# Adding DMAs for a weight sum only in the second and third part of each FFN, and another choice of groups with four pairs in seven products

## The chip, the cores and the metric

The kernel runs on one core of a Trainium2 chip, as one launch. Its time is the device time of that core in microseconds; of several runs the median is given. The engines are named as in the profile: PE (TensorE matmul) and PEld (its weight loads), DVE (VectorE), ACT (ScalarE), POOL (GpSimd) and SP (SyncE, which issues most of the DMAs).

## The reference

A decoder trunk of two layers over 256 positions of width 2048, all in float32. Each layer is a mixer and an FFN:

```python
for layer in range(DEPTH):
    xn = rms_norm(h, norm_mix[layer])
    mix = swa_mlstm_mixer(xn, ...) if layer % 2 == 0 else forgetting_attention_mixer(xn, ...)
    h = h + mix
    h = h + swiglu(rms_norm(h, norm_ffn[layer]), w_gate[layer], w_up[layer], w_down[layer])
return rms_norm(h, norm_final)

def swiglu(xn, w_gate, w_up, w_down):
    return (jax.nn.silu(xn @ w_gate) * (xn @ w_up)) @ w_down
```

The change is in `swiglu` alone: w_gate and w_up are 2048 x 5632, w_down is 5632 x 2048.

## The kernel before

**Products in halves.** A float32 weight chunk is split in two parts, `hi` (ACT casts it to fp32r) and `lo` (DVE: raw minus hi). So is the left side (`xh`, `xl` for the normed stream, `mh`, `ml` for the hidden values). A product is then three matmuls: hi with xh, lo with xh, hi with xl (`three`, lines 532 to 534). One weight chunk is 256 rows by 512 columns, 128 x 1024 in a tile.

**The FFN's walk.** The 5632 hidden columns are 11 groups of 512 (g = 0 to 10), in three parts: groups 0 to 2, 3 to 6 and 7 to 10 (`PARTS`). For each group `pair_group` computes the gate and the up columns together, over 16 blocks of 128 rows taken as eight pairs. When a part's groups are done, two further calls of `pair_group` multiply the hidden values of that part by w_down, two column blocks of 512 each (in the last part of the second FFN one such call, and two plain products).

**A pair in eight or in seven products.** For a pair of row blocks, two row tiles of positions and two matrices (gate and up) there are eight block products, 24 matmuls. That is a plain pair (kind 0 in the order tables). A pair of kind 1 is computed by a scheme with seven products, 21 matmuls, at the price of sums: of the left side (`sums_of`, made once and kept) and of the weights, which are made for every pair. The second matrix's first row block gets the first matrix's added to it; DVE then subtracts twice (lines 605 and 607), and ACT and DVE split four tiles instead of two (lines 187 and 188 for the raw gate chunk, 356 and 357 for the sums). At a group's end `combine` (lines 555 to 559) puts the four extra accumulators together.

`ORDER` has three pairs of kind 1 among eight, `HEAVY` has four (pairs 1, 3, 5 and 7, where pair 7 is `FOURTH`). A group whose number is in `DENSE` takes `HEAVY`. The down passes have two such pairs of six in part one (`DOWN[6]`) and three of eight in the others (`DOWN[8]`).

**Who makes the first sum.** The tile `ra` gets the gate chunk and `rb` the up chunk, by two plain DMAs that SP issues. The sum is then made by an adding DMA that POOL issues: it reads the same 128 x 512 of w_gate (in a down pass, of w_down's first column block) from memory once more and adds it to `rb` on the way in (line 599). It has to wait until the up chunk has landed; ACT's cast of `rb` (line 356) waits for it. `rb` and `ra` come from a pool of five tiles (`RAWS`), plain chunks from another one of four; the split parts go through eight pairs of tiles (`stock`), which PE empties.

**What sets the order.** The program is built by a planner that places the instructions of each engine by its own estimate of times; each engine then runs its own list strictly in that order. `run_due` puts some work at fixed places of a group: the copies that turn the normed residual stream for group 0 (`split_turned`, its `join` is line 322) and those that turn a group's hidden values (lines 703 and 710).

Of the kernel before, what the change touches and what calls it, by code (L numbers as in the profile page):

```python
# [12 lines left out]
ALU = mybir.AluOpType  # L13
# [10 lines left out]
NB = 512  # L24
# [11 lines left out]
ORDER = ((0, 0), (1, 1), (0, 2), (1, 3), (0, 4), (1, 5), (0, 6), (0, 7))  # L36
HEAVY = ((1, 1), (0, 0), (1, 3), (0, 2), (1, 5), (0, 4), (1, 7), (0, 6))
FOURTH = 7
DENSE = (1, 4, 5, 8, 9)
DOWN = {  # L40
    6: ((0, 0), (1, 1), (0, 2), (1, 3), (0, 4), (0, 5)),
    8: ((0, 0), (1, 1), (0, 2), (1, 3), (0, 4), (1, 5), (0, 6), (0, 7)),
# [33 lines left out]
def trunk(  # L76
# [19 lines left out]
    nc = tc.nc  # L96
# [58 lines left out]
    for n in (1, 2, 3):  # L155
# [8 lines left out]
        out=ident, in_=ident, pattern=[[-1, P]], compare_op=ALU.not_equal, fill=1.0, base=0, channel_multiplier=1  # L164
# [73 lines left out]
    sums = {}  # L238
# [116 lines left out]
    def split_plain(dst_h, dst_l, src):  # L355
        nc.scalar.copy(dst_h, src)  # L356
        nc.vector.tensor_tensor(out=dst_l, in0=src, in1=dst_h.bitcast(F32), op=ALU.subtract)  # L357
# [178 lines left out]
    def bank(par, name):  # L536
        return pm.tile([P, NB], F32, tag="pm", name=name) if par else pa.tile([P, NB], F32, tag="acc", name=name)

    def pair_group(fp, par, lhs, sums, mats, order, todo=(), halves=None, inner=None, raws=None):
        plain = [[bank(par, "acc") for _ in range(NT)] for _ in range(2)]  # L540
        begun = set()

        def fresh(*at):
            known = at in begun
            begun.add(at)
            return not known

        todo = list(todo)
        prods = None
        kinds = [kind for kind, _ in order]  # L550
        t0, t1 = slice(0, P), slice(P, 2 * P)

        def combine(prods):
            c = fp.tile([P, 4, NB], F32, tag="c", name="c", bufs=1)
            nc.scalar.copy(c[:, 0, :], prods[0])
            if halves is None:
                nc.vector.tensor_tensor(out=c[:, 1, :], in0=prods[3], in1=c[:, 0, :], op=ALU.add)
                nc.vector.tensor_tensor(out=c[:, 2, :], in0=prods[2], in1=c[:, 1, :], op=ALU.add)
                nc.vector.tensor_tensor(
                    out=c[:, 1:4:2, :],  # L560
                    in0=prods[1].rearrange("p (a n) -> p a n", a=1).broadcast_to([P, 2, NB]),
                    in1=c[:, 1:3, :],
                    op=ALU.subtract,
                )
                return c
            nc.vector.tensor_tensor(out=c[:, 2, :], in0=prods[3], in1=c[:, 0, :], op=ALU.add)
            nc.vector.tensor_tensor(out=c[:, 1, :], in0=prods[2], in1=c[:, 2, :], op=ALU.add)
            nc.vector.tensor_tensor(out=c[:, 3, :], in0=prods[1], in1=c[:, 1, :], op=ALU.subtract)
            nc.vector.tensor_tensor(out=c[:, 2, :], in0=prods[1], in1=c[:, 2, :], op=ALU.subtract)
            return c  # L570

        for pos, (kind, pair) in enumerate(order):
            k0 = 2 * pair
            if inner is not None and pos == len(order) - 1:
                c = combine(prods)
                inner()
            if not kind:
                last = pos == len(order) - 1
                walk = [(i, t) for i in range(CK) for t in range(NT)]
                if last:  # L580
                    walk.sort(key=lambda it: it[1])
                for m, (w, c0) in enumerate(mats):
                    hi, lo = load_chunk(w, k0, c0, NB)
                    run_due(todo, pos)
                    for i, t in walk:
                        ah, al = lhs(k0 + i)
                        ts = slice(t * P, (t + 1) * P)
                        three(
                            plain[m][t], ah[:, ts], al[:, ts], hi[:, i, :], lo[:, i, :],
                            fresh(m, t), last and i == CK - 1,  # L590
                        )
                continue
            first, last = 1 not in kinds[:pos], 1 not in kinds[pos + 1 :]
            if first:
                prods = [bank(1 - par, "prod") for _ in range(4)]
            ra, rb = (load_raw(w, k0, c0, NB, fp, W_RAWS if halves else RAWS, raws) for w, c0 in mats)
            if halves is None:
                (w, c0), part = mats[0], slice(k0 * P, (k0 + 1) * P)
                nc.gpsimd.dma_start(rb[:, 0, :], w[part, c0 : c0 + NB], accum_op=ALU.add)  # L599
            hg, lg = split_chunk(ra, NB)  # L600
            run_due(todo, pos)
            hu, lu = slot()
            if halves is None:
                split_plain(hu, lu, rb)
                nc.vector.tensor_tensor(out=rb[:, 1, :], in0=rb[:, 0, :], in1=rb[:, 1, :], op=ALU.subtract)  # L605
                both = rb[:, 1, :].rearrange("p (a n) -> p a n", a=1).broadcast_to([P, CK, NB])
                nc.vector.tensor_tensor(out=ra, in0=ra, in1=both, op=ALU.subtract)  # L607
                hc, lc = (a[:, 0, :] for a in slot())
                split_plain(hc, lc, rb[:, 1, :])
                hd, ld = slot()  # L610
                split_plain(hd, ld, ra)
                ht = [hu[:, 0, :], hd[:, 0, :], hc, hd[:, 1, :]]
                lt = [lu[:, 0, :], ld[:, 0, :], lc, ld[:, 1, :]]
            else:
                split_plain(hu[:, 1, :], lu[:, 1, :], rb[:, 1, :])
                nc.vector.tensor_tensor(out=ra[:, 0, :], in0=rb[:, 0, :], in1=ra[:, 0, :], op=ALU.add)
                nc.vector.tensor_tensor(out=rb[:, 0, :], in0=rb[:, 1, :], in1=rb[:, 0, :], op=ALU.subtract)
                nc.vector.tensor_tensor(out=rb[:, 1, :], in0=ra[:, 0, :], in1=rb[:, 1, :], op=ALU.subtract)
                nc.vector.tensor_tensor(out=ra[:, 1, :], in0=ra[:, 1, :], in1=rb[:, 1, :], op=ALU.subtract)
                parts = []  # L620
                for src in (ra, rb):
                    hs, ls = halves.pop(0)
                    halves.append((hs, ls))
                    split_plain(hs, ls, src)
                    parts.append((hs, ls))
                where = ((0, 0), (1, 0), (1, 1), (0, 1))
                ht = [parts[a][0][:, b, :] for a, b in where]
                lt = [parts[a][1][:, b, :] for a, b in where]
            sh, sl = sums(pair)
            xa, la = lhs(k0)  # L630
            xb, lb = lhs(k0 + 1)
            three(prods[0], xa[:, t0], la[:, t0], hg[:, 0, :], lg[:, 0, :], first, last)
            three(plain[0][0], xb[:, t0], lb[:, t0], hg[:, 1, :], lg[:, 1, :], fresh(0, 0), False)
            three(plain[1][0], sh[3], sl[3], hu[:, 1, :], lu[:, 1, :], fresh(1, 0), False)
            three(prods[1], sh[0], sl[0], ht[0], lt[0], first, last)
            three(prods[2], sh[2], sl[2], ht[1], lt[1], first, last)
            three(prods[3], sh[1], sl[1], ht[2], lt[2], first, last)
            three(plain[0][1], xb[:, t1], lb[:, t1], ht[3], lt[3], fresh(0, 1), False)
        if inner is None:
            c = combine(prods)  # L640
        return plain, c

    def ffn(layer, fp, sx, x4, sd, key, todo, idx_next=None, key_next=None, finish=None):
# [8 lines left out]
        for g0, g1 in zip(PARTS, PARTS[1:]):  # L652
            end = g1 == PARTS[-1]
            nk = 4 * (g1 - g0)
            order = DOWN[nk // 2]
            for g in range(g0, g1):
                par = (g1 - 1 - g) % 2
# [5 lines left out]
                    [(w_gate[layer], g * NB), (w_up[layer], g * NB)],  # L663
                    HEAVY if g in DENSE else ORDER,
                    todo,
                )
                todo = []
                for m in range(2):
# [79 lines left out]
            for n0 in (0, 2):  # L748
                if end and idx_next is None and n0 == 2:
                    for n in (2, 3):  # L750
                        acc = new_acc()
                        gemm(acc, m_of, wd, n * NB, NB, 0, nk, nk, skew=3 if n == 3 else 1, halved=n == 3)
                        close(acc, n)
                    continue
                plain, c = pair_group(
                    fp, 1 - n0 // 2, m_of, sums_d, [(wd, n0 * NB), (wd, (n0 + 1) * NB)], order, todo
                )
                todo = []
                if end and idx_next is None:
                    gf = fp.tile([P, D], F32, tag="c", name="gf", bufs=1)  # L760
                    nc.gpsimd.dma_start(gf, norm_final.partition_broadcast(P))
                for t in range(NT):
                    o = h[:, t, n0 * NB : (n0 + 2) * NB]
                    nc.vector.tensor_tensor(
                        out=o, in0=c[:, 2 * t : 2 * t + 2, :].rearrange("p a n -> p (a n)"), in1=o, op=ALU.add
                    )
                for m in range(2):
                    close(plain[m], n0 + m)
# [614 lines left out]
```

## Time and profile before

| | |
|---|---|
| median of 3 runs | 2097.1 us (2096.4 to 2097.92) |
| the profiled execution, its own time | 2095.33 us |
| its span, first to last instruction | 2093.6 us |
| busy: PE / PEld / DVE / ACT / POOL | 99% / 82% / 86% / 66% / 6% |
| mean granted clock of PE | 0.998 |
| adding DMAs (line 599) | 76 from w_gate, 29 from w_down, 256 KB each |
| DMA traffic | 462.43 MB, mean 221 GB/s |

Time before and after the span belongs to the launch. A row of a group reads: line, engine, operation, output<-inputs, count, busy time in us, mean ns of one, then the idle time of the engine just before these instructions and what ended most of it. Matmuls overlap, so a busy PE is not a PE at its full pace; how many matmuls a stretch held for its length tells more. In a table by stretch each engine has its busy time and, in brackets, how many instructions it began there; then come PE's granted clock, the DMA engines' busy share and GB/s.

### The profile page before, as it was taken

To read this page: it belongs to the slowest core of one execution; us is meant where nothing else is said; L and a number is where in the kernel's file an instruction comes from. 1 tells how busy PE (TensorE), PEld (TensorE's weight loads), DVE (VectorE), ACT (ScalarE), POOL (GpSimd) and SP (SyncE) were. 2 spreads that over 40 slices of the span, in tenths; PEclk is the share of its full clock that TensorE was granted. 3 is DMA by queue.
4 is the path that set the end of the run, shared out by engine and by line. 5 is a ranking of instruction groups with operands and counts; after the bars stand their busy time and mean duration, and the time that the engine had idled before them with its cause. 6 is when DMAs were issued, how large, how long until landed. Compare 5 with 4: busy or idle time off the path is not lost.

```text
span 2093.6 us, 27094 instructions
## 1 busy us (share of the span) xinstructions
PE 2072.1 (99%) x9443; PEld 1709.8 (82%) x9443; DVE 1794.4 (86%) x2217; ACT 1384.1 (66%) x1764; POOL 133.7 (6%) x171
## 2 busy tenths in 40 slices
PE   9999999999999999999999999999999999999998
PEld 8878887778888888888888888887788888888887
DVE  6788768988999998998899678578899999999995
ACT  6767677665567656667676776686655667557763
POOL 1010000000000000000000001000000000000000
PEclk9999999999999999999999999999999999999999
DMA  8666578777788777887676777597778777867864
GB/s 294 177 201 201 195 257 226 217 215 218 220 229 265 227 244 220 237 238 202 204 225 198 227 201 186 162 263 202 243 220 244 228 223 234 265 201 209 263 208 150
DMA packets 324698, 462.43 MB, mean 221 GB/s; under 512 B 108092, under 2 KB 116304, under 8 KB 324432
## 3 DMA queue, kind: packets, MB, share of 16 engines
q1 hardware_dynamic: 307088, 426.27, 64.8%
q0 software_dynamic: 16752, 33.33, 9.0%
q8 instruction: 74, 1.21, 0.2%
q10 hardware_dynamic: 720, 1.09, 0.1%
q14 instruction: 64, 0.52, 0.1%
HBM read 436.21 MB, written 2.12 MB: 209 GB/s over the span
## 4 chain that ended last, share of the span: by engine, by line
PE 75%; DVE 8%; DMA 6%; ACT 5%; issue 4%; SPq 0%; ACTq 0%; POOLq 0%; POOL 0%; DVEq 0%
PE acc L533 16%; PE acc L532 16%; PE acc L534 16%; PE prod L533 4%; PE prod L532 4%; PE prod L534 4%; PE acc L222 4%; PE acc L223 4%; PE acc L224 4%; DVE lo L188 2%; DVE lo L357 2%; DMA raw<-in_w_down_dram 2%; ACT hi L187 2%; DMA raw<-in_w_gate_dram 1%; ACT hi L356 1%
## 5 line engine op out<-in xcount | busy, mean ns | idle before, releaser
L188 DVE TENSOR_TENSOR lo<-raw,hi 128x1024 fp32r<-128x1024 f32 (+2 forms) x646 | 761.7, 1194 | 153.8 <-ACT hi L187 151.2
L187 ACT CAST hi<-raw 128x1024 fp32r<-128x1024 f32 (+2 forms) x646 | 651.6, 1026 | 319.8 <-PE acc L534 83.7
L533 PE MATMUL acc<-lo,xh 128*128 128x512 f32 x1260 | 491.7, 391 | 1.0 <-DVE lo L188 1.0
L534 PE MATMUL acc<-hi,xl 128*128 128x512 f32 x1260 | 490.1, 390 | 0.0
L532 PE MATMUL acc<-hi,xh 128*128 128x512 f32 x1260 | 478.6, 392 | 5.5 <-ACT hi L187 3.9
L356 ACT CAST hi<-raw 128x1024 fp32r<-128x1024 f32 (+1 forms) x329 | 291.4, 894 | 226.5 <-DVE raw L605 84.6
L357 DVE TENSOR_TENSOR lo<-raw,hi 128x1024 fp32r<-128x1024 f32 (+1 forms) x329 | 334.9, 1029 | 52.2 <-ACT hi L356 50.8
L532 PEld LDWEIGHTS acc<-hi,xh 128*128 128x128 f32 x1260 | 236.8, 188 | 58.8 <-ACT hi L187 7.7
L533 PEld LDWEIGHTS acc<-lo,xh 128*128 128x128 f32 x1260 | 236.8, 188 | 53.0 <-DVE lo L188 3.9
L534 PEld LDWEIGHTS acc<-hi,xl 128*128 128x128 f32 x1260 | 236.9, 188 | 48.9
L533 PE MATMUL acc<-lo,mh 128*128 128x512 f32 x466 | 181.6, 390 | 0.0
L534 PE MATMUL acc<-hi,ml 128*128 128x512 f32 x466 | 181.4, 389 | 0.0
L532 PE MATMUL acc<-hi,mh 128*128 128x512 f32 x466 | 175.8, 390 | 0.5 <-ACT hi L187 0.5
L607 DVE TENSOR_TENSOR raw<-raw 128x1024 f32<-128x1024 f32 x105 | 128.3, 1222 | 1.0
L599 POOL DMA_DIRECT2D raw<-in_w_gate_dram x76 | 65.1, 856 | 963.9 <-DMA raw<-in_w_up_dram 391.4
L223 PE MATMUL acc<-lo,mh 128*128 128x512 f32 (+1 forms) x322 | 126.3, 392 | 0.0
L222 PE MATMUL acc<-hi,mh 128*128 128x512 f32 (+1 forms) x322 | 125.8, 391 | 0.0
L224 PE MATMUL acc<-hi,ml 128*128 128x512 f32 (+1 forms) x322 | 123.7, 391 | 0.0
L532 PEld LDWEIGHTS acc<-hi,mh 128*128 128x128 f32 x466 | 87.5, 188 | 19.4 <-ACT hi L187 1.3
L533 PEld LDWEIGHTS acc<-lo,mh 128*128 128x128 f32 x466 | 87.5, 188 | 18.1
L534 PEld LDWEIGHTS acc<-hi,ml 128*128 128x128 f32 x466 | 87.5, 188 | 18.1
L223 PE MATMUL acc<-lo,xh 128*128 128x512 f32 (+3 forms) x288 | 99.7, 347 | 0.2 <-DVE lo L188 0.2
(361 smaller groups left out, 3093.3 us busy)
## 6 DMA issues: line engine op xcount, KB each, us to landing
raw<-in_w_gate_dram SPq DMA_DIRECT2D x176, 512.0 KB, 5.2
raw<-in_w_up_dram SPq DMA_DIRECT2D x176, 512.0 KB, 5.4
raw<-in_w_down_dram SPq DMA_DIRECT2D x176, 512.0 KB, 5.7
raw<-in_w_in_odd_dram SPq DMA_DIRECT2D x88, 512.0 KB, 5.3
raw<-in_w_in_even_dram SPq DMA_DIRECT2D x51, 512.0 KB, 4.8
raw<-in_w_gate_dram POOLq DMA_DIRECT2D x76, 256.0 KB, 5.7
raw<-in_w_out_even_dram SPq DMA_DIRECT2D x32, 512.0 KB, 5.4
raw<-in_w_out_odd_dram SPq DMA_DIRECT2D x32, 512.0 KB, 4.8
```

The source lines that it names most:

```text
L187: latest[0] = nc.scalar.copy(hi[:, k, 0:n], raw[:, k, 0:n])
L188: nc.vector.tensor_tensor(out=lo[:, k, 0:n], in0=raw[:, k, 0:n], in1=hi[:, k, 0:n].bitcast(F32), op=ALU.subtract)
L222: nc.tensor.matmul(o, ah[:, ts], hi, start=(k == 0), stop=False)
L223: nc.tensor.matmul(o, ah[:, ts], lo, start=False, stop=False)
L224: nc.tensor.matmul(o, al[:, ts], hi, start=False, stop=(k == k_all - 1 and cs.stop == n))
L356: nc.scalar.copy(dst_h, src)
L357: nc.vector.tensor_tensor(out=dst_l, in0=src, in1=dst_h.bitcast(F32), op=ALU.subtract)
L532: nc.tensor.matmul(o, ah, hi, start=start, stop=False)
L533: nc.tensor.matmul(o, ah, lo, start=False, stop=False)
L534: nc.tensor.matmul(o, al, hi, start=False, stop=stop)
L599: nc.gpsimd.dma_start(rb[:, 0, :], w[part, c0 : c0 + NB], accum_op=ALU.add)
L607: nc.vector.tensor_tensor(out=ra, in0=ra, in1=both, op=ALU.subtract)
```

## The change

In both FFNs:

- Part one (groups 0 to 2 and their down pass) has no adding DMA any more. DVE makes the sum, one 128 x 512 add of `ra` to `rb`, ahead of the split of `rb`. It reads two tiles that the plain DMAs fill. Parts two and three keep the adding DMA.
- Group 1 goes back to three pairs in seven products, and groups 3 and 7, the first ones of parts two and three, get four. So three groups with four such pairs follow each other in each of these parts: 3, 4, 5 and 7, 8, 9.

Counted over the kernel, 105 adding DMAs become 81, and 26 adds on DVE come. 28 adding DMAs leave part one (per FFN ten in the groups and four in the down pass), four come to parts two and three.

```diff
-DENSE = (1, 4, 5, 8, 9)
+DENSE = (3, 4, 5, 7, 8, 9)
+ADDING = 3
...
-    def pair_group(fp, par, lhs, sums, mats, order, todo=(), halves=None, inner=None, raws=None):
+    def pair_group(fp, par, lhs, sums, mats, order, todo=(), halves=None, inner=None, raws=None, adding=False):
...
             ra, rb = (load_raw(w, k0, c0, NB, fp, W_RAWS if halves else RAWS, raws) for w, c0 in mats)
-            if halves is None:
+            if adding:
                 (w, c0), part = mats[0], slice(k0 * P, (k0 + 1) * P)
                 nc.gpsimd.dma_start(rb[:, 0, :], w[part, c0 : c0 + NB], accum_op=ALU.add)
             hg, lg = split_chunk(ra, NB)
             run_due(todo, pos)
             hu, lu = slot()
             if halves is None:
+                if not adding:
+                    nc.vector.tensor_tensor(out=rb[:, 0, :], in0=ra[:, 0, :], in1=rb[:, 0, :], op=ALU.add)
                 split_plain(hu, lu, rb)
...
                     HEAVY if g in DENSE else ORDER,
                     todo,
+                    adding=g0 >= ADDING,
...
-                    fp, 1 - n0 // 2, m_of, sums_d, [(wd, n0 * NB), (wd, (n0 + 1) * NB)], order, todo
+                    fp, 1 - n0 // 2, m_of, sums_d, [(wd, n0 * NB), (wd, (n0 + 1) * NB)], order, todo, adding=g0 >= ADDING
```

Lines behind the change move down by one to four: 187, 322, 356 and 357 become 188, 323, 357 and 358; 599 becomes 600; the new add is 606, and 605 and 607 become 608 and 610; 671 and 675 become 675 and 679.

The planner's order changes with it. First POOL's list over the first FFN; `r` is the norm's factor and `st` work of the mixer before. Before:

```order
L1108 TENSOR_TENSOR st<-st,mhalf 128x2 x4
L599 DMA raw<-in_w_gate_dram 128x512 x3
L254 TENSOR_TENSOR r<-tot,mhalf 128x2
L599 DMA raw<-in_w_gate_dram 128x512 x7
L599 DMA raw<-in_w_down_dram 128x512 x4
L599 DMA raw<-in_w_gate_dram 128x512 x14
```

After:

```order
L1112 TENSOR_TENSOR st<-st,mhalf 128x2 x4
L255 TENSOR_TENSOR r<-tot,mhalf 128x2
L600 DMA raw<-in_w_gate_dram 128x512 x15
L600 DMA raw<-in_w_down_dram 128x512 x6
L600 DMA raw<-in_w_gate_dram 128x512 x15
```

The ten and four of part one are gone from POOL, and each later part has 15 instead of 14.

Next ACT's list in group 0 of the first FFN, around the copies that turn the last quarter of the normed stream (`box`); `hi_3096` and the like are fixed split tiles of `stock`. Before:

```order
L361 ACTIVATE xh<-box,gT 128x256 x4
L303 ACTIVATE full<-box,gT 128x256 x2
L187 COPY hi<-raw 128x1024 x3
L322 COPY box<-box 128x1024 x2
L356 COPY hi<-raw 128x512
L356 COPY hi<-raw 128x1024 x2
```

After:

```order
L362 ACTIVATE xh<-box,gT 128x256 x4
L304 ACTIVATE full<-box,gT 128x256 x2
L188 COPY hi<-raw 128x1024 x2
L357 COPY hi<-raw 128x512
L188 COPY hi<-raw 128x1024
L323 COPY box<-box 128x1024 x2
L357 COPY hi<-raw 128x1024 x2
```

The 128x512 cast of the sums (line 356, now 357) has moved ahead of the copies.

Last DVE's list at the end of group 0 and the start of group 1, from the sums of group 0's results (line 671, now 675) on. Before:

```order
L671 TENSOR_TENSOR c<-acc,c 128x512 x3
L357 TENSOR_TENSOR lo<-raw,hi 128x512
L607 TENSOR_TENSOR raw<-raw 128x1024
L675 TENSOR_SCALAR c<-c,r 128x512
L357 TENSOR_TENSOR lo<-raw,hi 128x1024
L188 TENSOR_TENSOR lo<-raw,hi 128x1024
```

After:

```order
L675 TENSOR_TENSOR c<-acc,c 128x512 x3
L608 TENSOR_TENSOR raw<-raw 128x512
L189 TENSOR_TENSOR lo<-raw,hi 128x1024
L679 TENSOR_SCALAR c<-c,r 128x512
L189 TENSOR_TENSOR lo<-raw,hi 128x1024
L610 TENSOR_TENSOR raw<-raw 128x1024
L358 TENSOR_TENSOR lo<-raw,hi 128x512
L679 TENSOR_SCALAR c<-c,r 128x512
L358 TENSOR_TENSOR lo<-raw,hi 128x1024 x2
L608 TENSOR_TENSOR raw<-raw 128x512
L606 TENSOR_TENSOR raw<-raw 128x512
L610 TENSOR_TENSOR raw<-raw 128x1024
```

The add of a pair (line 606) stands in DVE's list among the subtractions of the pair before it, with splits of other chunks behind it.

## The prediction

> **What bounds the kernel now.** I read the page first, then the busy time of each engine stretch by stretch, then the waits of PE and ACT in the stretches that stood out, and last single instructions there.
>
> ```profile
> span 2093.6 us, 27094 instructions
> ...
> PE 2072.1 (99%) x9443; PEld 1709.8 (82%) x9443; DVE 1794.4 (86%) x2217; ACT 1384.1 (66%) x1764; POOL 133.7 (6%) x171
> ...
> PE 75%; DVE 8%; DMA 6%; ACT 5%; issue 4%; SPq 0%; ACTq 0%; POOLq 0%; POOL 0%; DVEq 0%
> ```
>
> PE is the bound, DVE the next engine. In the chain that ended last 23% is not PE (8 + 6 + 5 + 4), so the question is where PE is fed late. The six stretches below are the gate/up groups of part one, two and three of the first FFN, then of the second; PEld counts the weight loads, one for each matmul.
>
> ```profile
> core 0: us, PE busy (x) PEld busy (x) DVE busy (x) ACT busy (x) POOL busy (x), PEclk, DMA share, GB/s
> 321.70:457.50 135.80, 131.46 (x556) 104.31 (x555) 116.88 (x145) 96.43 (x119) 9.27 (x11) 0.99 0.78 222
> 519.80:684.30 164.50, 164.50 (x727) 136.29 (x726) 155.93 (x176) 109.79 (x121) 11.95 (x14) 1.00 0.80 235
> 767.30:932.60 165.30, 164.89 (x727) 136.08 (x726) 153.85 (x174) 109.36 (x120) 11.95 (x14) 1.00 0.79 234
> 1388.20:1526.00 137.80, 132.31 (x556) 103.88 (x555) 117.23 (x146) 96.77 (x119) 9.28 (x11) 0.99 0.79 219
> 1588.10:1752.70 164.60, 164.60 (x728) 136.29 (x727) 153.86 (x173) 109.60 (x120) 11.95 (x14) 1.00 0.80 235
> 1835.70:2000.20 164.50, 164.50 (x727) 136.24 (x726) 153.46 (x172) 109.15 (x120) 11.95 (x14) 1.00 0.80 235
> ```
>
> Parts two and three run at 164.5 / 726 = 0.2266 us a matmul, and three of the four have no gap in PE at all. At that pace the 555 of part one would take 125.8 us. They take 135.8 and 137.8: **10.0 and 12.0 us lost, 22.0 in all**. Only 0.8 us is lost elsewhere in the FFN groups (165.3 against 164.5). Single groups of part one, with a group of each kind from the later parts:
>
> ```profile
> 321.70:365.40 43.70, 42.88 (x185) 33.96 (x184) 34.82 (x50) 34.30 (x50) 3.28 (x4) 1.00 0.82 222
> 365.40:411.90 46.50, 44.12 (x182) 34.75 (x181) 41.72 (x48) 32.64 (x36) 3.43 (x4) 0.96 0.76 218
> 411.90:457.50 45.60, 44.46 (x193) 35.59 (x192) 40.34 (x48) 29.49 (x34) 2.56 (x3) 1.00 0.76 226
> ```
> ```profile
> 849.60:891.20 41.60, 41.19 (x182) 33.58 (x181) 40.88 (x48) 29.49 (x34) 3.43 (x4) 1.00 0.86 256
> 519.80:561.30 41.50, 41.50 (x185) 34.38 (x184) 40.20 (x43) 24.30 (x27) 3.40 (x4) 1.00 0.75 228
> 561.30:602.10 40.80, 40.80 (x182) 33.80 (x181) 37.26 (x44) 28.87 (x32) 2.56 (x3) 1.00 0.74 217
> 457.50:519.80 62.30, 62.02 (x278) 51.03 (x277) 55.77 (x59) 32.19 (x37) 3.43 (x4) 1.00 0.74 221
> ```
>
> Group 0 loses 43.7 − 184 × 0.2266 = 2.0 us, group 1 (four pairs in seven products) 46.5 − 41.0 = 5.5, group 2 45.6 − 43.5 = 2.1. A group of the same form as group 1 takes 40.8 in part two (561.3). DVE is not full in part one (116.88 of 135.8), so something makes it wait. ACT's waits in part one, first FFN and then second:
>
> ```profile
> ACT hi L356 <- DMA raw<-in_w_gate_dram: 11.1, 2, 5.8
> ...
> ACT hi L187 <- DMA raw<-in_w_up_dram: 1.6, 1, 1.6
> ```
> ```profile
> ACT hi L356 <- DMA raw<-in_w_gate_dram: 9.0, 2, 5.7
> ...
> ACT hi L187 <- DMA raw<-in_w_up_dram: 3.0, 2, 2.3
> ```
>
> L356 casts the tile `rb`, whose plain load comes from w_up; what reaches it from w_gate is the adding DMA alone. So 20.1 us of ACT's waiting here is for adding DMAs, against 4.6 for the loads. One of them, in POOL, ACT and DVE:
>
> ```profile
> 360.10 0.84 POOL L599 DMA_DIRECT2D raw<-in_w_gate_dram  x1 [9.67 <-DVE lo L357]
> ```
> ```profile
> 365.37 1.57 ACT L356 CAST hi<-raw 128x1024 fp32r<-128x1024 f32 x2 [5.27 <-DMA raw<-in_w_gate_dram]
> ```
> ```profile
> 366.45 1.23 DVE L357 TENSOR_TENSOR lo<-raw,hi 128x1024 fp32r<-128x1024 f32 x1 [2.89 <-ACT hi L356]
> ```
>
> Issued at 360.10, landed at 365.3; ACT stands 5.27 us, DVE 2.89 behind it, with every later cast queued after them.
>
> **The change, part by part.** Rows for the prices:
>
> ```profile
> L188 DVE TENSOR_TENSOR lo<-raw,hi 128x1024 fp32r<-128x1024 f32 x610 | 737.1, 1223 | 144.2 <-ACT hi L187 141.7 <-DMA hv<-room 0.4 <-DMA raw<-in_w_gate_dram 0.2
> ...
> L357 DVE TENSOR_TENSOR lo<-raw,hi 128x1024 fp32r<-128x1024 f32 x210 | 254.6, 1223 | 42.6 <-ACT hi L356 41.2 <-DMA raw<-in_w_down_dram 0.7
> ...
> L607 DVE TENSOR_TENSOR raw<-raw 128x1024 f32<-128x1024 f32 x105 | 128.3, 1222 | 1.0
> ...
> L357 DVE TENSOR_TENSOR lo<-raw,hi 128x512 fp32r<-128x512 f32 x119 | 81.9, 688 | 9.6 <-ACT hi L356 9.6
> ...
> L605 DVE TENSOR_TENSOR raw<-raw 128x512 f32<-128x512 f32 x105 | 72.3, 689 | 1.0
> L599 POOL DMA_DIRECT2D raw<-in_w_gate_dram x76 | 65.1, 856 | 963.9 <-DMA raw<-in_w_up_dram 391.4 <-DVE lo L188 125.9 <-DVE raw L607 78.1
> ```
> ```profile
> DMA to landing us min/median/max: 4.1/5.9/8.6
> ```
>
> *Matmuls.* A pair in seven products has 21 matmuls, a plain one 24. Per FFN group 1 loses its fourth such pair (+3), groups 3 and 7 gain one (−6): −3, over two FFNs −6, all on PE, 6 × 0.2266 = **−1.4 us**.
>
> *Adding DMAs out of part one.* Per FFN 10 in gate/up (3 + 4 + 3) and 4 in down go; 9 + 4 adds on DVE come. Such an add has the form of L605: 0.689 us, so 26 × 0.689 = 17.9 us more on DVE in the whole kernel, and a latency of 0.7 us in place of one median 5.9 us behind POOL's queue. What hides the 17.9 is DVE's slack. A pair in seven products costs DVE 1.223 + 2 × 1.223 + 1.222 + 0.688 + 0.689 = 6.27 us, a plain one 2 × 1.223 = 2.45. Part one then needs 116.9 + 9 × 0.689 − 3.8 = 119.3 us of DVE in 555 + 3 matmuls = 126.4 us: 94%. Part two runs at 155.93 / 164.5 = 95% with no loss, so the cover holds on average; in the down pass it is 55.8 + 2.8 = 58.6 of 62.3. If it fails, all 13 × 0.689 = 9 us per FFN comes onto PE.
>
> The stall itself: groups 1 and 2 lose 5.5 + 2.1 = 7.6 us in the first FFN and, by the 12.0 and a like first group, about 9 in the second. These lie behind the 5 us waits quoted, and the add on DVE shortens each by 5. Bounds: all 16.6 gone, or none, if DVE turns late at the same places; I take 14, near the upper end, since loads made ACT wait only 4.6 us and parts two and three show DVE this full without loss. Group 0 loses 2.0 (about 3 in the second FFN), partly behind ACT's copies that turn the normed stream; ACT's list there now has one cast of a sum ahead of them. Between 0 and 5 I take half, 2.5. Together **−16.5 us**. Late next: group 0's own start, where nothing has been cast ahead.
>
> The new add waits for both loads on DVE, and behind it stand splits of other pairs, for which PE waits next; a late load would now stop DVE directly. The 4.6 us of load waits in the rows above bound that.
>
> *Three such groups in a row.* Parts two and three each get one more pair in seven products (+6.27 − 2.45 = 3.8 us DVE, one more adding DMA on POOL at 0.856 us to issue): DVE then has 155.93 + 3.8 = 159.7 in 163.8 us, 97.5%, at worst, 96% in the others. No row shows three in a row. Nearest: the second of two, 849.6 to 891.2, lost 0.8 with DVE at 40.88 of 41.6; the other three second ones nothing. Bounds: 0, or a loss like part one's. I take **+1.5 us** over four parts, since ACT still stands there for free buffers, that is, runs ahead of PE:
>
> ```profile
> ACT hi L187 <- PE acc L534: 2.5, 2, 2.1
> ```
>
> Sum: −1.4 − 16.5 + 1.5 = −16.4. The profiled execution took 2095.33 us (span 2093.6); the median shown is 2097.1, 1.8 above, so 2097.1 − 16.4 = **2080.7 us**.
>
> [...] The clock row is 0.96 in group 1, where PE was busy 44.12 of 46.5 us; the slow clock costs 0.04 × 46.5 = 1.9 us there, inside the 5.5. [...]
>
> **Rivals.**
> 1. *DVE takes the place of the DMA in part one.* Group 0 starts with nothing ahead and DVE has its own norm work; for it: DVE already works 41.72 of 46.5 in group 1. Against: 94% on average. Then about half the stall stays: −8 − 1.4 + 1.5, 2089 us.
> 2. *Slower: the third heavy group empties what was cast ahead.* If the third and the group after it lose as groups 1 and 2 of part one do (5.7 + 2.1 = 7.8 us against the undisturbed forms), four parts cost 31 us: 2097.1 − 17.9 + 31 = 2110. It outweighs the gain from 17.9 / 4 = 4.5 us a part. For it: 97.5%, the 0.8 us at 849.6, and the 5.9 us adding DMAs that remain there. Against: 0 us in three of four pairs of heavy groups.
> 3. *It all goes.* 22.0 + 1.4 off and no new loss: 2073.7.
> 4. *No effect.* The waits named after the add are really late loads or free buffers, so the add was hidden: only −1.4, about 2096.
>
> **Chances.** Forecast (2075 to 2086) 0.50, rival 1 (2086 to 2093) 0.19, rival 3 0.08, rival 4 and mixtures within 0.2% (4.2 us, about what these runs can tell apart) 0.05, rival 2 0.18. Faster 0.77, same 0.05, slower 0.18. The range leaves out rival 2 and little else: 2073 to 2098; the forecast's own is 2075 to 2086.
>
> **What would show it.** Part one at 127 to 130 us instead of 135.8 and 137.8, no wait of ACT L356 (now L357) on in_w_gate there, the clock at 1.00, DVE near 119 us; parts two and three at 163.8 to 164.5, with DVE 157 to 160. The prediction is wrong if PE waits on DVE in part one (rival 1), or if groups 5, 6, 9 and 10 stretch (rival 2).

## The result, and the profile after

The changed kernel took 2107.54 us (median of 9 runs, 2099.99 to 2109.34), the kernel before 2096.4 (9 runs on the same chip, 2095.45 to 2098.68): a ratio of 1.0043, 95% interval 1.0032 to 1.0053. It is slower by some 9 us (by the ratio) to 11 us (by the medians), where 16 less had been forecast. The profiled execution took 2104.77 us, 9.4 more than the one of before. Runs of the changed kernel at a mean granted clock of 0.995 to 0.996 took 2100.0 to 2104.8 us, those at 0.993 to 0.994 took 2107.5 to 2109.3, so the profiled one is among the faster.

The page of the changed kernel, its span, engines and chain of waits:

```profile
span 2103.1 us, 27010 instructions
...
PE 2072.6 (99%) x9437; PEld 1711.2 (81%) x9437; DVE 1819.7 (87%) x2251; ACT 1387.5 (66%) x1768; POOL 115.6 (5%) x147
...
PE 74%; DVE 9%; DMA 7%; ACT 5%; issue 4%; SPq 0%; ACTq 0%; POOL 0%; DVEq 0%; POOLq 0%
```

PE has its 6 matmuls less, POOL its adding DMAs, DVE 25 us more work. Nothing on this page says where the time went; DVE and DMA have a point more of the chain each. The busy time by stretch does (columns: start and end, length, then each engine's busy time and instructions, PE's granted clock, DMA share, GB/s). First the six stretches of groups as in the prediction, then groups 0, 1, 2 and the first down call of part one, and groups 4, 5 and 6:

```profile
322.00:453.60 131.60, 128.68 (x559) 105.39 (x558) 117.86 (x149) 95.15 (x117) 0.69 (x1) 0.99 0.69 208
519.50:688.20 168.70, 166.00 (x725) 136.52 (x724) 156.40 (x176) 109.34 (x121) 12.29 (x15) 0.99 0.80 232
771.10:939.70 168.60, 166.25 (x725) 136.69 (x725) 156.33 (x176) 109.49 (x121) 12.61 (x15) 0.99 0.80 231
1395.50:1525.20 129.70, 127.67 (x558) 104.25 (x557) 117.85 (x149) 95.29 (x117) 0.71 (x1) 1.00 0.71 211
1589.40:1757.30 167.90, 165.55 (x724) 135.32 (x723) 155.94 (x175) 109.48 (x121) 11.96 (x14) 1.00 0.80 235
1841.10:2009.10 168.00, 165.56 (x725) 135.27 (x724) 156.69 (x175) 109.37 (x121) 12.79 (x15) 1.00 0.80 233
...
322.00:368.70 46.70, 43.77 (x185) 35.27 (x184) 37.12 (x54) 36.38 (x52) 0.69 (x1) 0.96 0.72 203
368.70:410.20 41.50, 41.50 (x185) 34.38 (x184) 40.27 (x49) 29.73 (x33) 0.00 (x0) 1.00 0.69 215
410.20:453.60 43.40, 43.40 (x193) 35.75 (x192) 40.47 (x48) 29.04 (x34) 0.00 (x0) 1.00 0.65 206
453.60:488.20 34.60, 32.47 (x139) 26.34 (x138) 33.08 (x37) 17.27 (x21) 0.00 (x0) 0.95 0.57 183
...
560.30:601.10 40.80, 40.80 (x182) 33.79 (x180) 36.84 (x43) 27.64 (x31) 3.22 (x4) 1.00 0.78 226
601.10:646.70 45.60, 42.91 (x182) 34.55 (x181) 41.98 (x49) 29.41 (x33) 3.46 (x4) 0.96 0.78 227
646.70:688.20 41.50, 41.50 (x185) 34.38 (x184) 40.14 (x48) 28.76 (x32) 2.59 (x3) 1.00 0.85 248
```

Part one's groups went from 135.8 and 137.8 us to 131.6 and 129.7. Groups 1 and 2 have no gap in PE left. Group 0 takes 46.7 instead of 43.7, and the first call of the down pass, which had lost nothing, 34.6. Parts two and three went from about 164.7 to about 168.3 us each, although they have fewer matmuls: the third group with four pairs in seven products, group 5 here, takes 45.6 us where the second one, group 4, takes 40.8.

For the rest of this document "lost" means: the length of a group, from its first weight load to the next group's, less what a group of that form takes where PE has no gap (41.5 us; 40.8 with four pairs in seven products; 43.3 for group 2, which has some transposes; 31.3 for a down call of part one). Summed over both FFNs, from the one profiled execution of each kernel, in us:

| kernel (label of the experiment) | median, us | ratio to before, 95% | g0 | g1 | g2 | first down call of part one | g5 + g6 | g9 + g10 | other | all |
|---|---|---|---|---|---|---|---|---|---|---|
| before | 2096.4 | | 5.2 | 10.3 | 6.8 | 0 | 0 | 0.8 | 0 | 23.1 |
| after | 2107.5 | 1.0032 to 1.0053 | 8.3 | 0 | 0.3 | 5.0 | 8.8 | 8.8 | 0.7 | 31.9 |
| e1 | 2093.3 | 0.9976 to 0.9994 | 6.8 | 0 | 0 | 0 | 4.7 | 9.0 | 0 | 20.4 |
| e2 | 2084.8 | 0.9935 to 0.9960 | 3.8 | 0.4 | 5.3 | 1.5 | 0.8 | 0 | 0 | 11.7 |
| e3 | 2086.8 | 0.9947 to 0.9974 | 4.6 | 0 | 0.3 | 3.6 | 0 | 0 | 0 | 8.6 |
| e4 | 2104.1 | 1.0031 to 1.0056 | 5.6 | 0 | 0.4 | 5.2 | 10.1 | 8.4 | 0 | 29.6 |
| e5 | 2099.4 | 1.0005 to 1.0023 | 8.8 | 0 | 0.4 | 6.9 | 2.8 | 2.5 | 7.1 | 28.5 |
| e6 | 2127.9 | 1.0129 to 1.0161 | 9.0 | 2.2 | 3.7 | 2.8 | 1.8 | 1.5 | 4.6 | 25.6 |
| e7 | 2114.0 | 1.0072 to 1.0099 | 9.9 | 0 | 0.4 | 1.8 | 16.1 | 9.9 | 1.9 | 40.0 |
| e8 | 2094.2 | 0.9984 to 1.0002 | 5.2 | 0.3 | 10.9 | 3.1 | 0 | 0 | 0 | 19.5 |
| e9 | 2081.0 | 0.9919 to 0.9944 | 6.2 | 0 | 0 | 0 | 0 | 0 | 0 | 6.2 |
| e10 | 2086.9 | 0.9947 to 0.9972 | 2.5 | 0 | 3.4 | 0 | 0.9 | 1.5 | 6.7 | 15.1 |
| e11 | 2094.9 | 0.9986 to 1.0004 | 0.4 | 11.7 | 4.6 | 0 | 1.9 | 1.7 | 4.0 | 24.2 |
| e12 | 2088.3 | 0.9949 to 0.9977 | 8.8 | 0 | 0 | 0 | 0.7 | 1.5 | 5.8 | 16.9 |

After loses 8.8 us more than before; with 1.4 us of matmuls less that is 7.4 of the 9.4. The other 2.0 lie outside these groups, in small pieces.

What part one gained, by ACT's waits in its groups (322.0 to 453.6, first FFN; total, times, longest):

```profile
ACT hi L188 <- PE acc L535: 12.8, 6, 5.3
...
ACT hi L188 <- DMA raw<-in_w_gate_dram: 3.3, 1, 3.3
...
ACT hi L357 <- DVE raw L606: 0.5, 1, 0.5
```

The 11.1 us of L356 (now L357) behind adding DMAs are gone, and ACT now waits mostly for free split tiles; at those moments it is ahead of PE. So far the prediction's picture holds.

The stall of group 5, instruction by instruction (start, length, engine, line, idle before and what ended it):

```profile
606.62 2.96 DVE L358 TENSOR_TENSOR lo<-raw,hi 128x512 fp32r<-128x512 f32 x3
609.49 1.88 DVE L675 TENSOR_TENSOR c<-acc,c 128x512 f32<-128x512 f32 x3
611.29 0.68 DVE L608 TENSOR_TENSOR raw<-raw 128x512 f32<-128x512 f32 x1
...
604.47 1.05 ACT L357 CAST hi<-raw 128x1024 fp32r<-128x1024 f32 x1 [0.60 <-DVE raw L610]
610.21 0.72 ACT L677 ACTIVATE c<-c,r 128x512 f32<-128x512 f32 x1 [4.69 <-DVE c L675]
616.20 1.04 ACT L357 CAST hi<-raw 128x1024 fp32r<-128x1024 f32 x1 [3.50 <-DMA raw<-in_w_gate_dram]
...
611.80 0.86 POOL L600 DMA_DIRECT2D raw<-in_w_gate_dram  x1 [16.53 <-DVE c L675]
...
607.33 0.37 SPq L135 DMA_DIRECT2D raw<-in_w_up_dram  x1
...
617.30 0.69 PE L533 MATMUL prod<-hi,sx 128*128 128x512 f32 x1 [2.44 <-ACT hi L357]
```

Read backwards: PE stands 2.44 us for a cast; that cast waited 3.50 us for an adding DMA; POOL issued that DMA at 611.80, when the plain load issued at 607.33 had landed in the same tile (at 611.17; the row names DVE's L675, which ended at 611.37, but that writes another tile); and SP had waited with that load until DVE's L358 of 606.62 gave the tile back. Load (4.5 us to POOL's issue) and adding DMA (4.4 us to the cast) stand one behind the other, and both behind a tile that came free late. POOL had issued nothing for 16.5 us. In the group before, DVE worked 36.84 of 40.8 us: over a whole group it was not full, but from 606.6 on it works through its list, the sums at the end of group 4 (L675) among it, and ACT stands 4.69 us for one of those.

### The profile page after: what moved, and what is told of

It is laid out like the page before. It is cut to its first block, busy times and chain, and to the rows that moved or that the text cites. A ratio compares the mean times of both kernels' runs of the same rounds, so it can differ in the third digit from the quotient of the medians.

```text
span 2103.1 us, 27010 instructions
## 1 busy us (share of the span) xinstructions
PE 2072.6 (99%) x9437; PEld 1711.2 (81%) x9437; DVE 1819.7 (87%) x2251; ACT 1387.5 (66%) x1768; POOL 115.6 (5%) x147
## 4 chain that ended last, share of the span: by engine, by line
PE 74%; DVE 9%; DMA 7%; ACT 5%; issue 4%; SPq 0%; ACTq 0%; POOL 0%; DVEq 0%; POOLq 0%
PE acc L533 15%; PE acc L534 15%; PE acc L535 15%; PE prod L533 4%; PE prod L534 4%; PE prod L535 4%; PE acc L223 4%; PE acc L224 4%; PE acc L225 4%; DVE lo L189 3%; DMA raw<-in_w_down_dram 3%; ACT hi L188 2%; DVE lo L358 2%; DMA raw<-in_w_gate_dram 1%; DMA raw<-in_w_in_odd_dram 1%
## 5 line engine op out<-in xcount | busy, mean ns | idle before, releaser
L189 DVE TENSOR_TENSOR lo<-raw,hi 128x1024 fp32r<-128x1024 f32 (+2 forms) x644 | 758.7, 1193 | 142.2 <-ACT hi L188 138.5
L534 PE MATMUL acc<-lo,xh 128*128 128x512 f32 x1248 | 484.8, 390 | 0.0
L535 PE MATMUL acc<-hi,xl 128*128 128x512 f32 x1248 | 483.6, 390 | 0.0
L533 PE MATMUL acc<-hi,xh 128*128 128x512 f32 x1248 | 468.5, 392 | 3.8 <-ACT hi L188 3.0
L357 ACT CAST hi<-raw 128x1024 fp32r<-128x1024 f32 (+1 forms) x335 | 296.8, 893 | 183.0 <-DVE raw L608 55.7
L358 DVE TENSOR_TENSOR lo<-raw,hi 128x1024 fp32r<-128x1024 f32 (+1 forms) x335 | 339.7, 1027 | 46.1 <-ACT hi L357 45.5
L600 POOL DMA_DIRECT2D raw<-in_w_gate_dram x60 | 51.7, 861 | 933.4 <-DMA raw<-in_w_up_dram 546.0
L534 PEld LDWEIGHTS acc<-lo,mh 128*128 128x128 f32 x466 | 87.6, 188 | 18.5 <-DVE lo L189 0.3
```

The costliest lines, as they stand in the source:

```text
L189: nc.vector.tensor_tensor(out=lo[:, k, 0:n], in0=raw[:, k, 0:n], in1=hi[:, k, 0:n].bitcast(F32), op=ALU.subtract)
L533: nc.tensor.matmul(o, ah, hi, start=start, stop=False)
L534: nc.tensor.matmul(o, ah, lo, start=False, stop=False)
L535: nc.tensor.matmul(o, al, hi, start=False, stop=stop)
```

## Experiments

Every kernel below is planned anew, so that even a one-line edit gives the engines other lists elsewhere too. A difference of a microsecond or two in one group is not read for that reason.

**The two edits apart.** `e1_dense_only` has the other groups, and keeps the adding DMA in all parts:

```diff
-ADDING = 3
+ADDING = 0
```

> The groups with four pairs are those of the changed kernel (3, 4, 5, 7, 8, 9), all sums by adding DMAs as before. Theory A (in the third such group in a row a pair's load, adding DMA and cast come later than PE): groups 5 and 9 lose 4 to 5 us each as in the changed kernel, 17.5 us in all; part one, with three pairs in group 1, loses 12 to 22 as before or less; 2104 to 2113 us. Rival C (the stall in groups 5 and 9 comes from the planner's order after a part one without adding DMAs): groups 5 and 9 lose nothing, 2088 to 2096.

`e2_add_only` has the other edit, with the groups of the kernel before:

```diff
-DENSE = (3, 4, 5, 7, 8, 9)
+DENSE = (1, 4, 5, 8, 9)
```

> Adding DMAs only in parts two and three, groups with four pairs as before (1, 4, 5, 8, 9). Theory A: no group 5 or 9 is a third one, so parts two and three lose under 1 us; part one loses about the 13.6 us of the changed kernel in place of 22; 2087 to 2090 us. Rival B (DVE is full): group 1 with four pairs and DVE adds needs 40.3 + 3.8 + 0.7 = 44.8 us of DVE in 40.8, so it loses 4 us in each FFN, 2095 to 2098.

Measured: 2093.27 us (0.9985 of before) and 2084.83 (0.9948). Each edit alone makes the kernel faster, by 2.6 and 11.1 us (by the medians); together they make it slower by 9 to 11. Group 0, group 1 and group 9 of e1, which still has the adding DMA:

```profile
321.80:366.40 44.60, 42.90 (x184) 34.01 (x183) 36.10 (x52) 36.56 (x52) 3.28 (x4) 1.00 0.83 232
366.40:407.90 41.50, 41.50 (x185) 34.37 (x184) 38.65 (x45) 29.94 (x34) 2.58 (x3) 1.00 0.77 233
844.10:889.00 44.90, 43.13 (x182) 34.70 (x181) 41.13 (x48) 28.89 (x32) 3.42 (x4) 0.96 0.79 230
```

Groups 1 and 2 of e2:

```profile
365.70:406.70 41.00, 41.00 (x182) 33.69 (x181) 40.96 (x49) 31.80 (x34) 0.00 (x0) 1.00 0.72 231
406.70:452.70 46.00, 44.80 (x193) 35.48 (x192) 42.37 (x51) 29.67 (x33) 0.00 (x0) 1.00 0.63 197
```

In e1 group 1 has adding DMAs (POOL issues three) and loses nothing, because it no longer has its fourth pair in seven products. In e2 it has the fourth pair and loses almost nothing, because DVE adds, though DVE is then full (40.96 of 41.0 us); group 2 behind it still loses 5.3 us, and in the first FFN ACT waits there 5.1 us for one load of w_up. Part one of e1 loses 6.8 us, where theory A had 12 to 22, and so e1 comes out below the 2104 to 2113 of that theory, although groups 5 and 9 stall as it said. So the 17.1 us of groups 1 and 2 before came from the two together, and either remedy takes most of them away; they were counted on once and can be had once. The 17.6 us of groups 5 and 9 come with the groups: 13.7 of them are in e1, where no add was moved.

**No third group.** `e3_two_in_a_row` is the changed kernel with neither group 1 nor groups 3 and 7 among those with four pairs:

```diff
-DENSE = (3, 4, 5, 7, 8, 9)
+DENSE = (4, 5, 8, 9)
```

> Four pairs in seven products in groups 4, 5, 8, 9 only, adding DMAs as in the changed kernel. Four pairs become plain ones: 12 matmuls more, 2.7 us. Theory A: the 17.5 us of groups 5 and 9 go, 2107.5 - 17.5 + 2.7 = 2092.7. Rival C: the stalls stay, about 2110.

Measured: 2086.84 us, 0.996. Nothing is lost in parts two and three, as theory A said. The time is 5.9 us below what it said: group 0 and part one's first down call, where DVE adds and no edit was made, lose 4.6 and 3.6 us in place of 8.3 and 5.0.

**Is it the adding DMA of the third group?** `e4_third_by_dve` lets DVE make the sum in groups 5 and 9 of the changed kernel:

```diff
-                    adding=g0 >= ADDING,
+                    adding=g0 >= ADDING and g not in (5, 9),
```

> The changed kernel, but groups 5 and 9 make their sums on DVE (16 adds of 0.69 us more, 16 adding DMAs fewer). Theory A: what is late is load plus adding DMA, and the add on DVE saves some 4 us of it, so the stalls of groups 5 and 9 go: 2088 to 2092. Rival B: DVE is the bound there; 4 x 0.69 = 2.8 us more in each of four groups, 2113 to 2119.

Measured: 2104.14 us, 1.0043 of before, the same ratio as the changed kernel and outside both expectations. Groups 5 and 6 of the first FFN:

```profile
599.30:641.40 42.10, 41.58 (x182) 33.47 (x181) 39.95 (x46) 28.54 (x32) 1.72 (x2) 1.00 0.74 221
641.40:685.90 44.50, 43.02 (x185) 34.04 (x184) 39.66 (x48) 27.91 (x31) 2.58 (x3) 1.00 0.74 222
```

The loss of groups 5 and 9 falls from 17.6 to 6.5 and comes back in the next group, where it had been nothing (18.5 with it). So the adding DMA of the third group alone is not the cause; DVE, which works 39.7 of 44.5 us where PE stands, is not full either.

**In a row, or three in a part?** `e5_spread`:

```diff
-DENSE = (3, 4, 5, 7, 8, 9)
+DENSE = (3, 4, 6, 7, 8, 10)
```

> The changed kernel with the three groups of four pairs in seven products not in a row: 3, 4, 6 and 7, 8, 10. The work on every engine and the number of matmuls stay. Theory A, three in a row use up what was cast ahead: groups 5 and 9 (now plain) lose nothing, 6 and 10 under 1.5 us each, so most of the 17.5 us lost there goes: 2086 to 2092. Theory B, the sum of DVE's work in a part is too much (97.5%): the loss stays, only later, at groups 6, 10 or the down passes, 12 us or more: 2099 to 2107.

Measured: 2099.40 us, 1.0014. The work is the same, and groups 5, 6, 9 and 10 lose 5.3 us instead of 17.6. But 7.1 us are lost in the second down calls, mostly in this one of the first FFN:

```profile
975.20:1021.00 45.80, 43.30 (x185) 34.41 (x184) 39.40 (x48) 28.26 (x42) 0.86 (x1) 0.96 0.46 127
```

Together that is 12.4 us, and theory B had 12 or more, only later; the time, too, lies in its 2099 to 2107, some 6 us (by the ratios) to 8 us (by the medians) below the changed kernel where theory A asked for 15 to 21. So this run speaks for theory B: apart from each other, the three groups leave much of the loss to a place behind them. Whether DVE's work is what is short, as theory B has it, or the tiles that it gives back, this run can't tell; the next ones have the same work and more tiles.

**Tiles.** Pairs in seven products keep their two chunks in five tiles, room for two pairs and one chunk of a third. `e6_six_sums_tiles` gives it a sixth, for which the plain chunks' ring has three instead of four (here and in two other places that name this number):

```diff
-RAWS = 5
+RAWS = 6
...
-    wr = ctx.enter_context(tc.tile_pool(name="wr", bufs=4))
+    wr = ctx.enter_context(tc.tile_pool(name="wr", bufs=3))
```

> The changed kernel with six tiles instead of five for the chunks of pairs in seven products, and, since the room ends there, three instead of four for plain chunks. The same instructions. Theory A', the stall of group 5 begins with a tile that DVE gives back late, and load and adding DMA (4 + 4 us) come one after the other behind it: a sixth tile lets that load go 2 to 5 us earlier, the losses of groups 5 and 9 (17.5 us) fall under 6, 2090 to 2097. Theory B', DVE itself is behind there (no gap from 600 to 614 us): they stay over 12, 2100 to 2108. A new loss where only plain chunks run (the mixers) would be the price of the three tiles.

Measured: 2127.87 us, 1.0145. The loss of groups 5 and 9 is 3.3 us, as theory A' said, but the mixers, which live on the plain ring, are slower: the first FFN begins at 336.1 instead of 322.0 us, the second at 1429.0 instead of 1395.5. `e10_seven_sums_tiles` pays in another place, with seven tiles and one pair of split tiles less:

```diff
-RAWS = 5
+RAWS = 7
...
-            more = [[fp.tile(...) for a in ("hi", "lo")] for i in range(2)]
+            more = [[fp.tile(...) for a in ("hi", "lo")] for i in range(1)]
```

> The changed kernel with seven tiles instead of five for the chunks of pairs in seven products, and seven instead of eight pairs of tiles for split chunks (the same room); the plain chunks keep their four. Theory A' (loads and adding DMAs start too late because a tile comes back late): groups 5 and 9 lose under 5 in all instead of 17.5, the mixers are not disturbed, 2086 to 2094. Rival, what counts is how much has been cast ahead: with one pair of tiles less they lose 17 or more, 2105 to 2115.

Measured: 2086.85 us, 0.9959, where the changed kernel has 1.0043: some 18 us faster, by two numbers that change no instruction's work. Groups 5 and 9 of the first FFN, and what SP waited for in groups 3 to 5 (in the changed kernel, 519.5 to 646.7, and here, 512.3 to 635.9):

```profile
594.10:635.90 41.80, 41.56 (x182) 33.64 (x182) 39.60 (x46) 30.55 (x34) 3.48 (x4) 1.00 0.80 238
842.80:883.90 41.10, 41.10 (x181) 33.65 (x180) 38.06 (x44) 28.80 (x32) 3.45 (x4) 1.00 0.80 239
...
SPq L135 <- DVE lo L358: 42.6, 15, 9.5
...
SPq L135 <- DVE lo L358: 22.3, 14, 5.3
```

45.6 us have become 41.8 with the same adding DMAs (four from POOL), the same work on DVE and the same three groups in a row, and SP waits half as long for the tiles that L358 gives back (for the plain ones, which L189 gives back, 45.9 us in place of 34.8). So DVE's work in a part, which theory B blamed, does not by itself make these groups lose. The first down call of part one, where DVE adds, lost 5.0 and loses nothing now. Less can be cast ahead than before, so the number of split tiles was not what was short in these groups. One thing stays open here: with more tiles the planner gives DVE and ACT other lists in part two as well, and no run has more tiles under the changed kernel's lists, so the tiles and the order that they allow are not told apart. Other lists alone are no cure: e1, e4 and e7, each with five tiles, lose 13.7 to 26.0 us in groups 5, 6, 9 and 10. What it costs is seen in "other": 6.7 us, in pieces of 0.5 to 1.8, mostly in down calls of parts two and three. e11 below, with the groups of the kernel before, loses 4.0 there where e2 lost nothing, so this goes with the smaller stock of split tiles, or with the plan that it gives.

`e12_groups_only_seven` is e1 with the same tiles (`ADDING = 0` beside the diff of e10):

> Only the other groups (3, 4, 5, 7, 8, 9), the adding DMA in all parts, and seven tiles for the chunks of pairs in seven products with seven pairs of split tiles. The run with five and eight took 2093.3 and lost 13.7 us in groups 5 and 9 and 6.8 in group 0. If the tile that comes back late is the cause of the former, they go to 3 or less and group 0 stays or shrinks (it fell from 5.2 and 3.2 to 0.3 and 2.1 with seven tiles in the changed kernel): 2078 to 2083, level with or ahead of the fastest so far (2081.0). If the smaller stock of split tiles makes itself felt as in the down passes of that run (1 us here and there): 2084 to 2088.

Measured: 2088.33 us, 0.9963. Groups 5 and 9 lose 1.4 us where e1 lost 13.7; the small losses of the down calls come here too (5.8), and group 0 is at 8.8. That group 0 would shrink was wrong: e10's 2.5 did not come from the tiles alone.

**Part one.** `e7_down_adding_dma` keeps the adding DMA in the down pass of part one of the changed kernel:

```diff
-                    fp, 1 - n0 // 2, m_of, sums_d, [(wd, n0 * NB), (wd, (n0 + 1) * NB)], order, todo, adding=g0 >= ADDING
+                    fp, 1 - n0 // 2, m_of, sums_d, [(wd, n0 * NB), (wd, (n0 + 1) * NB)], order, todo, adding=True
```

> The changed kernel with the adding DMA kept in part one's down pass (its four adds on DVE per FFN go). Theory D, DVE's adds made the first down call of part one lose 3.3 and 1.7 us: it loses under 1 in all, and without the half clock after it 2099 to 2102. Rival, the loads and the copies that turn the hidden values are late there, whoever adds: 3 to 6 us stay, 2103 to 2107.

Measured: 2114.02 us, 1.0085, slower than the changed kernel too and outside both expectations. The down call itself did what was expected, 1.8 us lost in place of 5.0. But groups 5 and 6 of the new plan lose 16.1 in place of 8.8, with the same instructions there as in the changed kernel. That a plan with three groups in a row is this close to the edge is all that follows.

`e8_group2_adding_dma` takes e2 and gives group 2 and the down pass back to the adding DMA:

```diff
-ADDING = 3
+ADDING = 2
...
-                    adding=g0 >= ADDING,
+                    adding=g >= ADDING,
```

> The kernel before with DVE adding only in groups 0 and 1 (the one with four pairs in seven products); group 2, the down pass of part one and the later parts keep the adding DMA. Against the run that had DVE add in all of part one (2084.8), where group 2 lost 2.65 and 2.61 us and the first down call 0.74 twice with DVE full in group 1. If DVE's backlog makes group 2 lose, three adds (2.1 us) off it leave under 1.5 each: 2080 to 2083. If the adding DMA's wait makes it lose, as in the kernel before (2.3 and 4.5): 2084 to 2089.

(Its down pass of part one has `adding=True`.) Measured: 2094.23 us, 0.9993, slower than both cases had it, and group 2 loses 10.9 us, twice the 5.3 of e2. Group 2 of the first FFN, and what ACT waited for in it:

```profile
406.50:454.80 48.30, 46.36 (x192) 36.77 (x191) 43.08 (x51) 31.65 (x37) 2.56 (x3) 0.96 0.76 227
```
```profile
ACT hi L357 <- DMA raw<-in_w_gate_dram: 4.2, 1, 4.2
ACT c L677 <- DVE c L675: 4.1, 2, 3.6
```

Behind a group with four pairs the adding DMA does hurt, as the prediction had it, and an add on DVE helps there. That DVE's own backlog is what group 2 of e2 loses by does not fit: three adds less for DVE made it worse.

`e11_before_groups_seven` is e2 with seven tiles:

> The same seven and seven tiles with the groups of the kernel before (1, 4, 5, 8, 9) and DVE adding in part one, the fastest so far (2084.8, which lost 11.7 us in its FFN groups: group 0 1.9 twice, group 2 2.6 twice). If earlier loads are what part one lacks too, groups 0 and 2 lose under 5 in all: 2077 to 2082. If DVE (full in group 1 there) or the start of group 0 is the limit, 2083 to 2087. If the smaller stock of split tiles costs, 2087 to 2095.

Measured: 2094.88 us, 0.9995. Group 0 loses 0.4 us in all, but groups 1 and 2 lose 16.3: with DVE full in group 1, more tiles for loads are no help. In group 1 of the first FFN DVE works 44.98 of 46.5 us, and PE waits 4.0 us for its splits. That the pair of split tiles less is what turned 0.4 us of loss in group 1 into 11.7 is likely, but no run shows it alone. What is short in group 1 with DVE's adds and a fourth pair is DVE's time, and in parts two and three it is tiles.

**Neither edit.** `e9_no_four_in_one` is the kernel before with one number taken out, group 1's fourth pair:

```diff
-DENSE = (1, 4, 5, 8, 9)
+DENSE = (4, 5, 8, 9)
```

> The kernel before with one edit: group 1 has three pairs in seven products like groups 0 and 2 (groups with four: 4, 5, 8, 9). All adding DMAs stay. It has 6 matmuls more than the kernel before (+1.4 us). Theory C, the loss of part one came from group 1's fourth pair and adding DMAs together, and either is remedy enough: part one loses about 7 as in the first run (the same groups 0 to 2), 2084 to 2088, no slower than the same groups with DVE adding (2086.8). Rival, the adding DMAs alone make groups 1 and 2 late and DVE's adds are what helps: groups 1 and 2 still lose 8 or more over both FFNs, 2091 to 2096.

Measured: 2081.04 us, ratio 0.9932 (0.9919 to 0.9944), the fastest of all, 14.8 us ahead of the kernel before (2095.87 on the same chip); by the ratios some 23 ahead of the changed one. Groups 0, 1 and 2 of the first FFN, with ten adding DMAs:

```profile
323.10:368.00 44.90, 43.02 (x185) 34.05 (x185) 36.05 (x52) 36.49 (x52) 3.28 (x4) 1.00 0.84 227
368.00:409.50 41.50, 41.50 (x185) 34.37 (x184) 38.14 (x45) 29.79 (x34) 2.59 (x3) 1.00 0.79 230
409.50:452.80 43.30, 43.30 (x193) 35.85 (x192) 41.22 (x48) 29.76 (x35) 2.56 (x3) 1.00 0.78 238
```

Only group 0 loses anything, 6.2 us in both FFNs. Beside e3, which has the same groups and DVE's adds in part one, the adding DMA is some 6 us faster (0.9932 against 0.9960 of before, intervals apart): once group 1 has no fourth pair, DVE's adds bring nothing. The profiled executions show 2.4 us of the difference in the FFN groups, with 3.6 lost in e3's first down call and 1.6 more in e9's group 0; where the rest lies is not shown.

## Why the prediction was wrong

By the profiled executions the forecast was −16.4 us and the change made +9.4: 25.8 off. By the prediction's own steps:

- *Matmuls*, −1.4: the count is right, 9443 to 9437.
- *Groups 1 and 2*, −14: they lost 17.1 and lose 0.3, so 2.8 better than forecast. The waits named (ACT for adding DMAs) were the right ones and are gone. But the step gave the gain to the add on DVE; e1 and e9 have it with all adding DMAs in place. The cause was the fourth pair of group 1 together with the adding DMA, and the change removed both.
- *Group 0*, −2.5: it lost 5.2 and loses 8.3, 5.6 off. In the table it ranges from 0.4 to 9.9 among kernels whose group 0 has the same products, so it hangs on the plan more than on who adds; this was not settled.
- *The down pass*, hidden ("58.6 of 62.3"): 5.0 off. The cover was an average over both calls. The first call has DVE busy 33.08 of 34.6 us, and its chunks go through the same five tiles: with seven (e10) it loses nothing, with adding DMAs (e7) 1.8.
- ***Three such groups in a row*, +1.5: this is the step that failed.** Groups 5, 6, 9 and 10 lose 17.6 us where before lost 0.8: 15.3 off, more than half of the miss. It was rival 2's case in place and sign, at 4.4 us a part against the 7.8 that rival 2 gave, and it decided at less than the 4.5 named because part one gave less than hoped. The step looked at DVE's share (97.5%) and at ACT's waits for free split tiles, and took the latter as proof of a lead. Neither was the limit: DVE's work in these parts came out at 155.9 to 156.7 us, below the 157 to 160 named, and with the same work and more tiles the loss goes. Each pair in seven products holds two of five tiles for as long as load, adding DMA, casts and DVE's subtractions last, and a load can't be issued before a tile is given back (SP waited 42.6 us for L358's in groups 3 to 5 of the first FFN). Three builds with more tiles (e6, e10, e12) bring these groups from 17.6 and 13.7 us to 3.3, 2.4 and 2.2, two of them with a smaller stock of split tiles (all three with other lists for the engines, too). Why the second such group in a row is still free and the third is not, the runs don't show instruction by instruction; e4, where the loss moves one group on, and e5, where a plain group between lets 7.1 of it come up only in a later down call, would fit a reserve that each such group uses up a little more.
- The rest, 2.7 us, is in a second down call (0.7) and outside the FFN groups (2.0).

Could the profile of before have told? SP's queue, which the prediction did not read, waited there for tiles just as it did after. The second group with four pairs before (849.6 to 891.2), which lost 0.8 us:

```profile
SPq L134 <- DVE lo L357: 13.6, 6, 9.5
```

Group 5 after (601.1 to 646.7), which lost 4.8:

```profile
SPq L135 <- DVE lo L358: 12.8, 6, 5.0
```

So that row shows that loads go only when DVE gives a tile back, that is, that there is no tile in reserve; it does not show how near the edge that is. It was a reason to widen the bound of this step, and no more.

Rival 1 (DVE takes the DMA's place in part one) was half right: it is what e2 shows, with DVE at 40.96 of 41.0 us in group 1, though that group loses only 0.4 by it; why group 2 of e2 still loses 5.3 is not settled. In the changed kernel group 1 had lost its fourth pair, and DVE had room.

The clock went with the stalls. Before, the granted clock was 0.96 in group 1 of the first FFN (365.4 to 411.9) and in group 2 of the second (1479.9 to 1526.0). After, it is 1.00 in groups 1 and 2 of both FFNs and lower where stalls are new or longer, all in the first FFN: 0.96 in group 0, 0.95 in the first down call, 0.96 in groups 5 and 9 each. In every one of these six groups and calls the trace has one stretch of 3.41 us at 0.50, so four instead of two. The 1.9 us that the prediction put down to the slow clock, inside the 5.5 of group 1, went with that group's stall and came back at other places.

## What to carry to other kernels

Two edits that cure the same stall are worth the stall once, not twice; run each alone, and the change that takes out the cause, before both. A share of busy time, even group by group, does not show a ring of buffers running out: look whether the transfer queue waits for buffers to be given back, and then count what comes one after the other from there to the first use (here a load of 4.5 and an adding DMA of 4.4 us). Before trusting such a stretch with more work, try it with a buffer more. An engine seen waiting for free room downstream at some moments of a stretch may still be late at others.

## What the runs showed of the hardware

PE's granted clock and its work around the stall of group 5 in the changed kernel, where it stood at 0.50 from 617.41 to 620.83, in four stretches of that length, and in two around a shorter stall in the second FFN:

```profile
610.60:614.00 3.40, 3.40 (x16) 2.82 (x15) 3.40 (x6) 0.96 (x2) 0.86 (x1) 1.00 0.66 170
614.00:617.41 3.41, 0.97 (x5) 0.49 (x3) 1.17 (x3) 1.21 (x2) 0.00 (x0) 1.00 0.67 135
617.41:620.83 3.42, 3.17 (x7) 2.18 (x8) 3.42 (x4) 3.42 (x4) 0.86 (x1) 0.50 0.22 83
620.83:624.24 3.41, 3.41 (x15) 2.60 (x15) 2.77 (x3) 3.41 (x5) 0.00 (x0) 1.00 1.08 163
...
1682.37:1685.78 3.41, 2.43 (x11) 1.69 (x9) 1.56 (x3) 0.40 (x1) 0.00 (x0) 1.00 0.65 93
1685.78:1689.20 3.42, 2.28 (x8) 1.37 (x9) 2.75 (x3) 3.42 (x5) 0.85 (x1) 1.00 0.35 131
```

PE worked 0.97 of the 3.41 us from 614.00 (it stood 2.44 us before its matmul at 617.30), and in the next 3.42 us the granted clock was 0.50: 7 matmuls in place of the 15 of the stretch after it. That makes the pause dearer by about 0.50 × 3.42 = 1.7 us, an estimate from these rows. Around the shorter stall, where PE stood 1.68 us before its matmul at 1686.47, it worked 2.43 and 2.28 us of the two stretches, and the clock was 1.00 in both. What decides whether the clock goes down after a pause is not shown.
